# Key weights of a decoder's second memory: loaded by GpSimd's queue into eight buffers of the queries' ring and split by GpSimd in turn with ScalarE and VectorE

## The chip, the core and the metric

The kernel runs on one core of a Trainium2 chip. The time is the device time of one execution in microseconds (us). The core has TensorE (PE in the profile, with its weight loads as PEld), VectorE (DVE), ScalarE (ACT), GpSimd (POOL) and SyncE (SP), which in this kernel issues the DMAs. Each engine works through its own queue in order; an instruction waits at the head of its queue until the semaphores that it needs have been raised.

## What is computed

A decoder trunk of two layers over 1024 tokens of width 1024. Each layer projects its input, runs a main path (causal pooling in layer 0, forgetting attention in layer 1) and a cross-attention of 4 heads into 256 memory tokens, gates both, projects back and normalizes. The part that matters here is the cross-attention's keys and values, computed in both layers from the same memory tokens with each layer's own weights:

```
def memory_attention(q_mem, mem, w_mem_kv):
    mkv = mem @ w_mem_kv
    mk = mkv[..., :D_MEM].reshape(B, M, MEM_HEADS, MEM_HEAD_DIM)
    mv = mkv[..., D_MEM:].reshape(B, M, MEM_HEADS, MEM_HEAD_DIM)
    q = q_mem.reshape(B, S, MEM_HEADS, MEM_HEAD_DIM)
    logits = jnp.einsum('bshd,bmhd->bhsm', q, mk) * (MEM_HEAD_DIM ** -0.5)
    p = jax.nn.softmax(logits, axis=-1)
    return jnp.einsum('bhsm,bmhd->bshd', p, mv).reshape(B, S, D_MEM)

x = layer_norm(ALPHA * x + y, ln_g[layer], ln_b[layer])    # at the end of each layer
```

The second memory of the title is that of layer 1: same tokens, second set of weights.

## The kernel before

Products are made at nearly float32 precision from three products of parts. A float32 operand is split (`hi_lo`, L159) into a high part (fp32r, a copy by ScalarE, L162), a low part (bf16, source minus high, by VectorE, L163) and a top part (bf16, a copy by ScalarE, L164). `three` (L153) pairs them: high with high, top with low, low with top. `gp_hi_lo` (L166) makes the same three parts on GpSimd alone (L157, L168); in this kernel it is used in layer 1's attention (`low[0]`). A weight block of 128 x 512 is loaded into a buffer `raw` (a ring of 4) by SyncE and split into ring `w` (6 buffers, so 3 split blocks) by `split_w` (L171).

At the end of layer 0, `OutProj.rest` (L457) goes over four pairs of row blocks. For each pair it runs three product groups of 48 products (L441) in the order 2, 0, 1; group 2 reads weights that lie in the buffers "B" of the first pool `in0`, group 1 reads some that lie in its buffers "Y". `norm` (L481) then normalizes the two row blocks on VectorE (L490 to L503), stores them, and leaves eight transposes per row block in the list `turns`. `spread` (L301) lets TensorE run one of them between other products; each four fill a PSUM bank "T", from which `hi_lo` writes the layer's output X1 (buffers "A"), the input of layer 1.

Layer 1 begins with `mem_kv(1)` (L609). It loads the memory tokens in four blocks into `raw` and splits them into buffers "T". `mem_attention` (L309) then projects the four heads' keys at once (L313 to L315, `keys`, `project`, L238): 24 products of 128 x 256 for each head (L248), with the last transposes of layer 0 spread among them. Each head needs two halves of weights (pc = 0 and 1, 256 KB each), loaded and split by `split_w`. Odd heads take the parts in the order top, low, high, even heads in the order high, top, low. The products gather in one of two PSUM banks "pj", emptied by a `hi_lo` into `mk` (buffers "MK"). Then the first input slab of layer 1 follows (`slab`, L193, products L214).

The queries and, later, much else of layer 1 lie in the ring `xy` (L600): ten buffers "B" of 4 KB per partition in the second pool, `in1`. Pool `in1` is opened after `in0` is closed and takes over its space; within a pool the space is laid out in the order in which the tags are first asked for, in `in0` "Y" (4 buffers), "B" (8) and "W" (4). A buffer that takes over space waits for whatever last read or wrote it. The order of instructions in each queue is set when the program is built, by the framework's own scheduler, except where `manual_schedule` fixes TensorE's order (after the slabs of the memory attention, and in the main attention of layer 1).

Of the kernel before, what the change touches and what calls it, by code (L numbers as in the profile page):

```python
# [10 lines left out]
F32R = mybir.dt.float32r  # L11
BF16 = mybir.dt.bfloat16
# [6 lines left out]
P = 128  # L19
# [6 lines left out]
MH = 4  # L26
# [46 lines left out]
def trunk_kernel(ctx, tc, x, xT, memT, win, wk, wv0, wv, wmk, wmv, wout, poolw, pscale, lng, lnb, bforget, out):  # L73
# [5 lines left out]
    nc = tc.nc  # L79
# [14 lines left out]
    def nm(tag):  # L94
        count[0] += 1
        return f"{tag}{count[0]}"

    def sb(shape, tag, bufs, dt=F32, where=None):
        return (where or pool).tile(shape, dt, tag=tag, name=nm(tag), bufs=bufs)

    def ps(shape, tag, bufs):
        return psum.tile(shape, F32, tag=tag, name=nm(tag), bufs=bufs)
# [7 lines left out]
    def MK(shape, dt=F32R):  # L110
        return sb(list(shape), "MK", 4, dt)

    def raw(shape):
        return sb(list(shape), "raw", 4)
# [35 lines left out]
    def parts_of(make, shape):  # L150
        return Split(make(shape), make([shape[0], 2] + list(shape[1:]), BF16))

    def three(a, b):  # L153
        return (a.hi, b.hi), (a.top, b.lo), (a.lo, b.top)

    def gp_copy(to, src):
        nc.gpsimd.tensor_scalar(to, src, 1.0, 1.0, ALU.mult, ALU.mult)  # L157

    def hi_lo(to, src, pinned=False, top=None):  # L159

        pin = tc.keep_in_program_order if pinned else lambda ins: ins
        pin(nc.scalar.copy(to.hi, src))  # L162
        pin(nc.vector.tensor_tensor(to.lo, src, to.hi.bitcast(F32), ALU.subtract))  # L163
        (top or nc.scalar.copy)(to.top, src)  # L164

    def gp_hi_lo(to, src):  # L166
        gp_copy(to.hi, src)
        nc.gpsimd.tensor_tensor(to.lo, src, to.hi.bitcast(F32), ALU.subtract)  # L168
        gp_copy(to.top, src)

    def split_w(src_dram, shape):  # L171
        r = raw(shape)
        nc.sync.dma_start(r, src_dram)
        to = parts_of(wt, shape)
        (gp_hi_lo if low[0] else hi_lo)(to, r)
        return to
# [49 lines left out]
        nc.scalar.activation(dst, acc, AF.Tanh, scale=0.5)  # L226
        nc.vector.scalar_tensor_tensor(dst, dst, 1.0, acc, ALU.add, ALU.mult)

    def mem_kv(l):

        ms = [parts_of(T, [P, 4, NMEM]) for _ in range(2)]
        for q in range(4):
            r = raw([P, 2, NMEM])
            nc.sync.dma_start(r, memT[:, 2 * q : 2 * q + 2, :])
            hi_lo(ms[q // 2][:, 2 * (q % 2) : 2 * (q % 2) + 2, :], r)
        mk, projected = parts_of(MK, [P, MH, NMEM]), []

        def project(w_dram):  # L238

            acc = ps([P, NH], "pj", 2)[:, :NMEM]  # L240
            ws = [split_w(w_dram[pc], [P, 4, P]) for pc in range(2)]
            parts = (1, 2, 0) if len(projected) % 2 else (0, 1, 2)
            projected.append(acc)
            for i in parts:
                for pc in range(2):
                    w, m = three(ws[pc], ms[pc])[i]
                    for k in range(4):
                        nc.tensor.matmul(  # L248
                            acc, w[:, k, :], m[:, k, :],
                            start=(i, pc, k) == (parts[0], 0, 0), stop=(i, pc, k) == (parts[2], 1, 3),  # L250
                        )
                        if k % 3 == 0:
                            spread()
            return acc

        two, v = (MK([P, MH, 2 * 2, P], F16) for _ in range(2))
        undo = const.tile([P, 8], F32, tag="undo", name=nm("undo"), bufs=1)[:, :MH]

        def keys(h):
            hi_lo(mk[:, h, :], project(wmk[l, h]))  # L260

        def vals(h):
            scaled_halves(
                project(wmv[l, h]), [two[:, h, 2 * e : 2 * e + 2, :].rearrange("p m t -> p (m t)") for e in range(2)],
                undo[:, h : h + 1],
            )
            if h == MH - 1:
                nc.sync.dma_start_transpose(v.rearrange("p h b d -> p (h b) d"), two.rearrange("p h b t -> p (h b t)"))

        return (mk, v, undo), keys, vals  # L270

    def scaled_halves(u, halves, un, by_tile=lambda t: t):

        m, e, sc = (tiny(1) for _ in range(3))
        nc.vector.tensor_reduce(m, u, AX.X, ALU.max, apply_absolute_value=True)
        nc.vector.tensor_scalar(m, m, 2.0 ** -100, None, ALU.max)
        nc.vector.tensor_scalar(e.bitcast(I32), m.bitcast(I32), 0x7F800000, None, ALU.bitwise_and)
        nc.vector.reciprocal(sc, e)  # L280
        nc.vector.tensor_scalar(sc, sc, 2.0 ** 14, None, ALU.mult)
        nc.vector.tensor_scalar(un, e, 2.0 ** -15 / PSCALE, None, ALU.mult)
        (hi, lo), u = halves, by_tile(u)
        nc.scalar.activation(hi, u, AF.Copy, scale=sc)
        nc.vector.scalar_tensor_tensor(lo, u, sc, hi, ALU.mult, ALU.subtract)
# [15 lines left out]
    def spread():  # L301

        if turns:
            turns.pop(0)()
# [232 lines left out]
    with tc.tile_pool(name="in0", bufs=1) as in0:  # L537
# [47 lines left out]
        out_proj = OutProj(0, w_slots(wtags, in0), y0d)  # L585
        pool_group(0)
        kv = mem_kv(0)
        mem_attention(0, X, kv, bt, lambda: sb([P, S], "Y", 4, F32, in0), y0d[2])
        for g in range(1, 4):
# [8 lines left out]
    with tc.tile_pool(name="in1", bufs=1) as in1:  # L598
# [7 lines left out]
        def vt(shape, dt=F32R):  # L606
            return sb(shape, "V", 4, dt, in1)

        kv = mem_kv(1)  # L609
        mem_attention(1, X, kv, xy, lambda: vt([P, S], F32), y1d[2])  # L610
        cumd = dram.tile([HEADS, S], F32, name="cumd")
        fg = G((P, 8, ST * HEADS))
# [118 lines left out]
        def pair_units(p):  # L731

            yield from qk_units(p)
            if p >= 2:
                u = MK([P, S], F32)
                yield from slab(wv[p - 2], X, lambda cols, acc: nc.scalar.copy(u[:, cols], acc))
            pairs[p].append(first_vs[p] if p < 2 else values_of(u))
# [214 lines left out]
        with tc.manual_schedule(engines={PE}):  # L952
            own, following = pair_units(0), pair_units(1)
# [66 lines left out]
```

## Time and profile before

| | |
|---|---|
| median of 3 runs | 1219.99 us (1217.21 to 1220.11) |
| profiled execution | 1218.15 us, its span 1216.4 us |
| TensorE busy | 1193.7 us (98%) |
| VectorE busy | 793.3 us (65%) |
| ScalarE busy | 697.4 us (57%) |
| GpSimd busy | 221.0 us (18%), nothing between the load of x and 601 us |
| DMA | 178.68 MB, all loads and stores on one queue (q1), issued by SyncE |

The page shows one execution. Rows of a timeline have the start, the duration, the engine, the line, the operation and the tiles written and read; x is how many follow each other, and a bracket gives the idle time ahead and what ended it. Rows of a group have the count, then busy time and mean duration in ns, then the idle time before and what ended it. Rows of one tile have minimum, median and maximum. The mean granted clock is 0.997 of full speed.

### The profile page before, as it was taken

The numbers are of one execution on the slowest core, as the hardware profiler recorded it, in microseconds if no ns is written. First come the engines' busy times: TensorE is split into PE (matmuls) and PEld (weight loads), VectorE is DVE, ScalarE is ACT, GpSimd is POOL, SyncE is SP. The second block draws the span as 40 slices with busy tenths as digits, with TensorE's granted clock in tenths as the row PEclk, the third lists the DMA queues.
The fourth block names the chain that finished last, engine by engine and source line by source line (L and its number), as shares of the span: only waits on it lengthen the run. The fifth ranks groups of instructions, "written<-read, shape, count | busy, mean of one in ns | idle before, by whom it ended". The sixth has DMA issues, their size and how long they took to land. (4 is left out here: it accounts for less than half of the span.)

```text
span 1216.4 us, 20026 instructions
## 1 busy us (share of the span) xinstructions
PE 1193.7 (98%) x7018; PEld 758.7 (62%) x7018; DVE 793.3 (65%) x1853; ACT 697.4 (57%) x1474; POOL 221.0 (18%) x349
## 2 busy tenths in 40 slices
PE   9999999999999998999999999999999999999996
PEld 4566666555555666667686666666666666665553
DVE  7534676475644457357736888878877888874754
ACT  6556774374542345567533777767776777685220
POOL 4000000000000000000002454544444434640000
PEclk9999999999999999999999999999999999999999
DMA  6232553232452333234517879988887989895340
GB/s 229 84 112 95 122 131 139 95 121 88 164 182 104 111 129 116 70 96 109 159 52 181 162 161 194 181 187 172 182 195 159 193 188 229 222 241 195 132 156 36
DMA packets 267414, 178.68 MB, mean 147 GB/s; under 512 B 212272, under 2 KB 225712, under 8 KB 267312
## 3 DMA queue, kind: packets, MB, share of 16 engines
q1 hardware_dynamic: 267312, 177.40, 56.2%
q8 instruction: 55, 0.90, 0.3%
q14 instruction: 47, 0.39, 0.1%
HBM read 94.97 MB, written 22.61 MB: 97 GB/s over the span
## 5 line engine op out<-in xcount | busy, mean ns | idle before, releaser
L214 PE MATMUL pj<-A,w 128*128 128x512 bf16 (+1 forms) x2928 | 684.7, 390 | 3.1 <-DVE B L724 1.6
L214 PEld LDWEIGHTS <-w 128*128 128x128 bf16 x1984 | 182.3, 98 | 223.8 <-issue 23.3
L214 PEld LDWEIGHTS pj<-A,w 128*128 128x128 f32 x976 | 181.1, 189 | 45.8 <-ACT A L162 2.8
L789 ACT ACTIVATE T<-MK,s 128x512 f32<-128x512 f32 x192 | 111.3, 580 | 41.5 <-DVE s L781 23.6
L811 DVE SCALAR_TENSOR_TENSOR P<-T,s,P 128x512 f16<-128x512 f32 x192 | 111.6, 613 | 34.7 <-ACT P L810 33.4
L163 DVE TENSOR_TENSOR w<-raw,w 128x512 bf16<-128x512 f32 x106 | 75.6, 714 | 83.6 <-PE pj L214 51.5
L810 ACT ACTIVATE P<-T,s 128x512 f16<-128x512 f32 x192 | 103.0, 576 | 46.0 <-ACT T L789 20.1
L441 PEld LDWEIGHTS <-T 128*128 128x128 bf16 x736 | 70.7, 98 | 82.9 <-issue 3.7
L191 PE MATMUL L<-B,B 128*128 128x512 f32 (+3 forms) x384 | 105.8, 381 | 2.2 <-DVE s L781 2.1
L686 POOL MEMSET G<- 128x128 f32 x1 | 0.2, 208 | 581.5 <-ACT MK L164 581.5
L191 PEld LDWEIGHTS L<-B,B 128*128 128x128 f32 x384 | 70.8, 189 | 22.9 <-DVE s L781 4.8
L162 ACT CAST w<-raw 128x512 fp32r<-128x512 f32 x106 | 65.9, 621 | 26.6 <-PE pj L214 14.6
L157 POOL TENSOR_SCALAR w<-raw 128x512 fp32r<-128x512 f32 x108 | 67.3, 629 | 65.0 <-PE pj L214 59.7
L781 DVE CUSTOM_DVE_ANT_0 MK<-L,R 128x512 f32<-128x512 f32 (+3 forms) x128 | 72.5, 566 | 8.7 <-PE L L191 6.9
L164 ACT CAST w<-raw 128x512 bf16<-128x512 f32 x106 | 65.7, 620 | 18.9 <-PE pj L214 18.2
L773 POOL TENSOR_SCALAR_AFFINE_SELECT R<-R 128x128 f32<-128x128 f32 x128 | 41.3, 328 | 174.4 <-DVE s L781 129.4
L168 POOL TENSOR_TENSOR w<-raw,w 128x512 bf16<-128x512 f32 x54 | 69.6, 1288 | 18.7 <-PE pj L214 16.2
L163 DVE TENSOR_TENSOR T<-T,T 128x1024 bf16<-128x1024 f32 x23 | 28.0, 1218 | 52.2 <-ACT T L162 36.9
L833 PE MATMUL O<-T,V 128*64 128x128 f16 (+1 forms) x1152 | 57.6, 220 | 2.7 <-DMA T<-P 2.5
L833 PEld LDWEIGHTS <-V 128*64 128x64 f16 (+1 forms) x1152 | 50.2, 104 | 15.2 <-issue 5.7
L162 ACT CAST T<-T 128x1024 fp32r<-128x1024 f32 x23 | 24.1, 1046 | 60.3 <-DMA T<-y1d 33.9
L441 PE MATMUL pj<-B,T 128*128 128x512 bf16 (+1 forms) x192 | 52.6, 383 | 0.0
(230 smaller groups left out, 1699.3 us busy)
## 6 DMA issues: line engine op xcount, KB each, us to landing
raw<-in_win_dram SPq DMA_DIRECT2D x96, 256.0 KB, 2.8
raw<-in_wout_dram SPq DMA_DIRECT2D x40, 256.0 KB, 2.8
B<-B SPq DMA_DIRECT2D x32, 256.0 KB, 4.2
R<-cumd SPq DMA_DIRECT2D x16, 512.0 KB, 5.0
y0d<-Y SPq DMA_DIRECT2D x12, 512.0 KB, 3.1
T<-y0d SPq DMA_DIRECT2D x12, 512.0 KB, 3.8
T<-y1d SPq DMA_DIRECT2D x11, 512.0 KB, 4.9
raw<-in_wmk_dram SPq DMA_DIRECT2D x16, 256.0 KB, 2.6
```

The lines of the kernel that those rows point to most:

```text
L157: nc.gpsimd.tensor_scalar(to, src, 1.0, 1.0, ALU.mult, ALU.mult)
L162: pin(nc.scalar.copy(to.hi, src))
L163: pin(nc.vector.tensor_tensor(to.lo, src, to.hi.bitcast(F32), ALU.subtract))
L168: nc.gpsimd.tensor_tensor(to.lo, src, to.hi.bitcast(F32), ALU.subtract)
L191: nc.tensor.matmul(acc, a, b, start=i == 0, stop=i == len(terms) - 1)
L214: nc.tensor.matmul(accs[n], a[:, k, :], b[:, pc * 4 + k, n * NH : (n + 1) * NH], start=seen[n] == 1, stop=seen[n] == 3 * KT,)
L441: nc.tensor.matmul(accs[a][nh], y, w, start=kt == 8 and i == 0, stop=kt == 7 and i == 2,)
L781: nc.vector.tensor_tensor_reduce(p[:, lo:up], lg, R[:, lo:up], 1.0, top, ALU.add, ALU.min, m[:, n : n + 1])
L789: nc.scalar.activation(e, p[:, lo:up], AF.Exp, bias=top, scale=-1.0, accum_out=sums[:, n, hd % 2, i : i + 1],)
L810: nc.scalar.activation(pair[:, lo:up], e, AF.Copy, scale=r)
L811: nc.vector.scalar_tensor_tensor(pair[:, L + lo : L + up], e, r, pair[:, lo:up], ALU.mult, ALU.subtract)
L833: nc.tensor.matmul(acc[rows, (i % 4) * P : (i % 4) * P + P], v[:, b, 2 * j : 2 * j + (1 if e else 2), :].rearrange("p e d -> p (e d)"), pt ...
```

## The change

For layer 1 alone, `mem_kv` is given the ring `xy` (`own`). Three things change.

The top parts of the memory tokens are copied by GpSimd (`gp_copy`) instead of ScalarE.

The eight halves of key weights get buffers of their own: `ahead` takes eight buffers of ring `xy`, two for each head (one for the high parts of both halves, one for their low and top parts). They no longer pass through ring `w`. It is called before any key is projected. It loads the eight halves by GpSimd's queue in place of SyncE's, three loads ahead of the split, still through the four `raw` buffers.

Even halves are split by GpSimd alone (`gp_hi_lo`), odd halves by ScalarE (high), VectorE (low) and GpSimd (top). `keys` hands the split weights to `project`, which then loads none. The products and their number are the same.

```diff
-    def mem_kv(l):
+    def mem_kv(l, own=None):
 
         ms = [parts_of(T, [P, 4, NMEM]) for _ in range(2)]
         for q in range(4):
             r = raw([P, 2, NMEM])
             nc.sync.dma_start(r, memT[:, 2 * q : 2 * q + 2, :])
-            hi_lo(ms[q // 2][:, 2 * (q % 2) : 2 * (q % 2) + 2, :], r)
+            hi_lo(ms[q // 2][:, 2 * (q % 2) : 2 * (q % 2) + 2, :], r, top=gp_copy if l else None)
         mk, projected = parts_of(MK, [P, MH, NMEM]), []
 
-        def project(w_dram):
+        def ahead():
+
+            src = [wmk[l, h, pc] for h in range(MH) for pc in range(2)]
+            heads = [(own([P, 2, 4, P], F32R), own([P, 2, 2, 4, P], BF16)) for _ in range(MH)]
+            to = [Split(hi[:, pc], pair[:, pc]) for hi, pair in heads for pc in range(2)]
+            rs = []
+            for k in range(3 + len(src)):
+                if k < len(src):
+                    rs.append(raw([P, 4, P]))
+                    nc.gpsimd.dma_start(rs[k], src[k])
+                n = k - 3
+                if n >= 0 and n % 2:
+                    hi_lo(to[n], rs[n], top=gp_copy)
+                elif n >= 0:
+                    gp_hi_lo(to[n], rs[n])
+            return [to[2 * h : 2 * h + 2] for h in range(MH)]
+
+        def project(w_dram, ws=None):
 
             acc = ps([P, NH], "pj", 2)[:, :NMEM]
-            ws = [split_w(w_dram[pc], [P, 4, P]) for pc in range(2)]
+            ws = ws or [split_w(w_dram[pc], [P, 4, P]) for pc in range(2)]
...
+        early = ahead() if own else None
+
         def keys(h):
-            hi_lo(mk[:, h, :], project(wmk[l, h]))
+            hi_lo(mk[:, h, :], project(wmk[l, h], early and early[h]))
...
-        kv = mem_kv(1)
+        kv = mem_kv(1, xy)
```

In the built program the queues of all engines hold the same instructions in the same order as before outside this stretch, from the split of the memory tokens to the start of layer 1's first slab.

## The prediction

> **What bounds the kernel now.** I first read the page's engine totals, then its busy time by stretches, then TensorE's timeline where a stretch is not full.
>
> ```profile
> span 1216.4 us, 20026 instructions
> PE 1193.7 (98%) x7018; PEld 758.7 (62%) x7018; DVE 793.3 (65%) x1853; ACT 697.4 (57%) x1474; POOL 221.0 (18%) x349
> ```
>
> TensorE is busy 98% of the span, so a change elsewhere pays only where TensorE waits. Cut into 20 us, the only unfilled stretch of this neighbourhood is the one where layer 0 hands over to layer 1:
>
> ```profile
> 440.00:460.00 20.00, 20.00 (x98) 12.44 (x97) 8.20 (x13) 9.85 (x18) 0.00 (x0) 1.00 0.38 125
> 460.00:480.00 20.00, 16.05 (x111) 12.74 (x110) 17.07 (x37) 12.76 (x29) 0.00 (x0) 0.91 0.31 94
> 480.00:500.00 20.00, 20.00 (x113) 13.17 (x112) 7.96 (x18) 10.90 (x22) 0.00 (x0) 1.00 0.40 118
> ```
>
> Columns: stretch, length, busy time and count of PE, PEld, DVE, ACT, POOL, granted clock, DMA share, GB/s. From 460 to 480 TensorE idles 3.95 us, its clock averages 0.91, and GpSimd does nothing. TensorE's timeline there:
>
> ```profile
> 462.18 0.59 PE L441 MATMUL pj<-Y,T 128*128 128x512 bf16 x2
> 462.62 0.59 PE L441 MATMUL pj<-MK,T 128*128 128x512 bf16 x2
> 463.07 3.94 PE L248 MATMUL pj<-T,w 128*128 128x256 f32 x33
> 467.31 1.06 PE L294 MATMUL T<-ident,G 128*128 128x128 f32 x8 [0.29 <-DVE s L493]
> 470.99 1.65 PE L248 MATMUL pj<-T,w 128*128 128x256 f32 x7 [2.29 <-ACT w L162]
> 478.54 0.61 PE L248 MATMUL pj<-T,w 128*128 128x256 bf16 x4 [0.67 <-ACT w L164]
> 479.85 2.43 PE L248 MATMUL pj<-T,w 128*128 128x256 bf16 x20 [0.70 <-ACT w L164]
> 482.12 10.76 PE L214 MATMUL pj<-A,w 128*128 128x512 f32 x48
> 492.72 2.88 PE L248 MATMUL pj<-T,w 128*128 128x256 f32 x24
> 495.35 4.91 PE L214 MATMUL pj<-A,w 128*128 128x512 f32 x21
> ```
>
> The out-projection of layer 0 ends at 463.1, the 96 key products (L248) run until the first slab of layer 1 starts at 482.12: a stage of 19.05 us. Undisturbed, 24 such products take 495.35 - 492.72 = 2.63 us, 0.11 each, so 96 need 10.5 us, and the 16 transposes (8 in 1.06) 2.1 us. The stage thus holds 6.4 us that is not TensorE's work. That is the most the change can win. What ends the waits are ScalarE's splits of key weights (L162, L164); TensorE pays some more in the half clock behind the 2.29 us wait:
>
> ```profile
> 470.00:472.00 2.00, 1.01 (x6) 0.81 (x6) 2.00 (x5) 2.00 (x5) 0.00 (x0) 0.82 0.00 0
> 472.00:474.00 2.00, 2.00 (x11) 2.00 (x11) 1.65 (x3) 0.93 (x2) 0.00 (x0) 0.50 0.89 255
> 474.00:476.00 2.00, 2.00 (x16) 1.96 (x15) 1.48 (x3) 1.39 (x4) 0.00 (x0) 0.82 0.88 252
> ```
>
> **Part 1: when the new buffers may be written.** The eight buffers are the first of ring B in the second pool, whose space the first pool used. There tag Y was asked for before tag B, so the first four new buffers lie where Y lay. Those four Y buffers hold weights of the out-projection's last product group. In the built program GpSimd's first copy into a key buffer does wait for TensorE's last product that reads Y: the row at 462.18, whose second product ends at 462.77. So nothing is split ahead. Before, three of the eight halves lay ready in ring w by then:
>
> ```profile
> 444.45 0.69 DVE L163 TENSOR_TENSOR w<-raw,w 128x512 bf16<-128x512 f32 x1 [2.80 <-ACT w L162]
> 448.46 0.69 DVE L163 TENSOR_TENSOR w<-raw,w 128x512 bf16<-128x512 f32 x1 [1.17 <-ACT w L162]
> 453.63 0.68 DVE L163 TENSOR_TENSOR w<-raw,w 128x512 bf16<-128x512 f32 x1
> ```
>
> The last four new buffers lie over old B, free long before, but their writers stand behind the first ones in GpSimd's queue.
>
> **Part 2: GpSimd's chain.** In that queue, from 462.8: per head three copies and one subtraction (the even half whole, the odd half's top), with loads between. Durations, from the later layer where GpSimd splits the same shape:
>
> ```profile
> L168 POOL TENSOR_TENSOR w<-raw,w 128x512 bf16<-128x512 f32 x54 | 69.6, 1288 | 18.7 <-PE pj L214 16.2 <-POOL w L157 0.3
> L157 POOL TENSOR_SCALAR w<-raw 128x512 bf16<-128x512 f32 x54 | 34.3, 636 | 0.0
> L157 POOL TENSOR_SCALAR w<-raw 128x512 fp32r<-128x512 f32 x54 | 33.6, 622 | 65.0 <-PE pj L214 59.7 <-issue 5.1
> 674.83 1.28 POOL L168 TENSOR_TENSOR w<-raw,w 128x512 bf16<-128x512 f32 x1
> 676.07 0.62 POOL L157 TENSOR_SCALAR w<-raw 128x512 bf16<-128x512 f32 x1
> 676.64 0.29 POOL L773 TENSOR_SCALAR_AFFINE_SELECT R<-R 128x128 f32<-128x128 f32 x1
> ```
>
> Start to start a copy is 676.64 - 676.07 = 0.57 us, a subtraction 676.07 - 674.83 = 1.24. A head is 3 x 0.57 + 1.24 = 3.0 us; an even half 2.4.
>
> The first four loads take over the raw buffers of the memory tokens, whose last split on VectorE is
> ```profile
> 451.82 1.29 DVE L163 TENSOR_TENSOR T<-raw,T 128x512 bf16<-128x512 f32 x2 [2.66 <-PE T L294]
> ```
>
> so they are issued by about 455 and land under the out-projection. The other four reuse these buffers again and stand inside the chain: the fifth behind head 0, the sixth and seventh behind head 1, the eighth behind head 2's even half. What GpSimd pays for an issue no row shows; no load in this trace is GpSimd's. The nearest rows:
>
> ```profile
> 467.19 0.33 SPq L504 DMA_DIRECT2D x<-G  x1
> raw<-in_wmk_dram SPq DMA_DIRECT2D x16, 256.0 KB, 2.6
> ```
>
> Lower end: SyncE's 0.33 us for an issue. Upper end: 2.6, the whole load, as if GpSimd stood still until it landed. Between them I take 1.0, the mean of GpSimd's own copy (0.62) and subtraction (1.29), since it must do the issue as work of its own. The Trainium skill, "DMA: Bandwidth & Descriptors", section "Latency and other measured facts", puts about 1 us before the first byte for GpSimd's software path against about 0.6 for SyncE's; with an estimate of 1 us per issue its sum would be the same.
>
> So the eighth load is issued from 462.8 + 3.0 + 1.0 + 3.0 + 2 x 1.0 + 2.4 = 474.2, and lands 1.0 + 2.6 later, at 477.8.
>
> **Part 3: who waits for it.** ScalarE's queue in the built program then holds: the high copy of that load, the copy of the last-but-one transposed block, then the top part of head 0's keys, which frees TensorE's bank pj for head 2. Rows:
>
> ```profile
> 475.58 0.62 ACT L164 CAST w<-raw 128x512 bf16<-128x512 f32 x1
> 474.60 0.59 ACT L162 CAST A<-T 128x512 fp32r<-128x512 f32 x1 [0.48 <-PE T L294]
> 477.06 0.40 ACT L164 CAST MK<-pj 128x256 bf16<-128x256 f32 x1
> ```
>
> That is 0.62 + 0.59 + 0.40 = 1.6, so head 2 starts at 479.4; heads 2 and 3 are 48 products, 5.3 us. The first slab starts at 484.7 instead of 482.12: **+2.6 us**. GpSimd's last piece (head 3's odd top, behind the issue, head 2's odd top and head 3's even half: 474.2 + 1.0 + 0.6 + 2.4 + 0.6 = 478.8) is ready before head 3 needs it, and the last norm's output, held back on VectorE by the split of the sixth load, is transposed near 477: neither is last. With 0.33 per issue the same sum gives 484.7 - 4 x 0.67 = 482.0, no change; with 2.6 it gives 484.7 + 4 x 1.6 = 491.1, +9.
>
> **Part 4: GpSimd beside VectorE.** VectorE is at its fullest here (17.07 of 20). GpSimd's copies elsewhere are longer where VectorE subtracts at the same time:
>
> ```profile
> L157 POOL TENSOR_SCALAR MK<-B x2: 613/835/1057, 1046.9 to 1048.5; 128x512 bf16<-128x512 f32 x2
> L157 POOL TENSOR_SCALAR A<-T 128x1024 bf16<-128x1024 f32 x7 | 11.8, 1707 | 1.5 <-DMA T<-in_xT_dram 1.5
> ```
>
> A disturbed copy is 1.06 against 0.61, 0.44 of the 0.69 of a VectorE subtraction, 64% of it. While GpSimd's chain runs to 474.2, VectorE has such operations (two large inputs, neither from a product): one scale of 1.27, two of 0.74, three key splits of 0.69, 4.8 us:
>
> ```profile
> 465.89 1.27 DVE L503 SCALAR_TENSOR_TENSOR G<-G,s,P 128x1024 f32<-128x1024 f32 x1
> 467.55 0.74 DVE L501 SCALAR_TENSOR_TENSOR G<-G,s,P 128x512 f32<-128x512 f32 x1
> ```
>
> Lower end 0 (as if they never met), upper end 4.8 (each holds GpSimd up for its whole length). I take 64%, **+3.1 us**. The Trainium skill, "SBUF — State Buffer", section "Who interferes with whom", says that a VectorE instruction with two SBUF inputs and a GpSimd one that reads SBUF fully block each other; that speaks against this change, and by it the sum is nearer the upper end, an estimate of +2.6 + 4.8 = +7.4. The 1707 ns copy above agrees with it.
>
> **Part 5: what is taken away.** ScalarE loses the tops of the memory tokens (4 x 0.62) and of all key weights and half the high parts; VectorE loses half the subtractions. From 440 to 463 TensorE was full, so this frees nothing on the path; in the stage it is what made the 3.95 us of waiting, and the sum above already lets ScalarE start at once. Half clock: the trace lost 2 x (0.18 + 0.50 + 0.18) = 1.7 us to it (the three rows of 2 us above); the new waits of TensorE (near 474 to 476 and 477 to 479) are like the old one, so I change nothing, with -1.7 to +1.7 for the range. After the first slab the queues hold the same instructions in the same order as before, so what the stage loses is not won back: TensorE is full.
>
> **Sum.** +2.6 + 3.1 = **+5.7 us**. The profiled execution took 1218.15 us (span 1216.4), which would become 1223.9; it lies 1.84 under the median of 1219.99, to which I add the same: **1225.7**.
>
> **The rivals.** (a) Cheap: issues cost 0.33 and GpSimd is not disturbed. For it: 54 subtractions of GpSimd average 1288 ns beside a busy VectorE. Against it: the disturbed copies above. With both the sum is 0; with one alone it is +2.6 or +3.1: 1220 to 1223. (b) The change does what its words say: the weights lie ready at 463, and only TensorE's work is left. For it: GpSimd idle, the space of old B free. Against: the wait on Y. Up to -6.4, 1213.6; half of it is 1216.8. (c) GpSimd stands still until each load lands, 2.6 per issue: +9 and with disturbance to +14, 1229 to 1234. For it: nothing; against: SyncE's own queue shows an issue at 0.33 and a landing at 2.6 apart. It decides from about 2 us per issue.
>
> **Chances.** The forecast's own case, +3.7 to +9: 0.64; (a) 0.25; (b) 0.05; (c) 0.06. The bound of what can be told from no change is 0.3%, 3.7 us: slower 0.64 + 0.06 = 0.70, the same 0.25, faster 0.05. The range leaves out (b), the part of (a) in which the half clock is won back too, and most of (c): lower end 1219.5, half a microsecond under no change; upper end 1219.99 + 2.6 + 4.8 + 4 x 0.3 (an issue at 1.3) + 1.7 = 1230.3, about 1231.
>
> **What would show it.** Right: GpSimd's first key copy starts at 462.8, not near 441; the first slab starts near 487.8; ScalarE's split of the eighth load ends the wait before head 2; GpSimd's copies of the first two heads exceed 0.62; its gaps at the loads are about 1 us. Wrong: key copies before 463, or a first slab before 484.

## The result, and the profile after

The changed kernel takes 1226.18 us (median of 6 runs, 1225.18 to 1227.65); six runs of the kernel before, beside them, have a median of 1218.88 us. The ratio is 1.0061, 95% interval 1.0048 to 1.0074: slower by 7.3 us, where +5.7 was forecast. The profiled execution took 1225.53 us. The page's totals after:

```profile
span 1223.8 us, 20029 instructions
PE 1196.5 (98%) x7018; PEld 760.2 (62%) x7018; DVE 795.5 (65%) x1849; ACT 688.6 (56%) x1458; POOL 243.3 (20%) x377
```

The span grew by 7.4 us. TensorE's timeline of the stage after (in the changed file the out-projection's product is L460, the key product L265, the transpose L313):

```profile
462.79 0.59 PE L460 MATMUL pj<-Y,T 128*128 128x512 bf16 x2
463.22 0.59 PE L460 MATMUL pj<-MK,T 128*128 128x512 bf16 x2
...
464.14 1.67 PE L265 MATMUL pj<-T,B 128*128 128x256 f32 x12 [0.22 <-POOL B L157]
466.56 1.05 PE L265 MATMUL pj<-T,B 128*128 128x256 bf16 x8 [0.74 <-POOL B L157]
469.31 0.61 PE L265 MATMUL pj<-T,B 128*128 128x256 bf16 x4 [1.71 <-POOL B L157]
472.00 0.39 PE L265 MATMUL pj<-T,B 128*128 128x256 bf16 x1 [2.07 <-POOL B L157]
472.19 1.91 PE L313 MATMUL T<-ident,G 128*128 128x128 f32 x8
...
479.96 0.63 PE L313 MATMUL T<-ident,G 128*128 128x128 f32 x4 [1.43 <-ACT w L162]
481.52 1.08 PE L313 MATMUL T<-ident,G 128*128 128x128 f32 x4 [0.94 <-DVE G L522]
482.26 6.72 PE L265 MATMUL pj<-T,B 128*128 128x256 f32 x48
488.82 1.55 PE L214 MATMUL pj<-A,w 128*128 128x512 f32 x6
```

The out-projection ends at 463.22 + 0.59 = 463.81 (463.21 before) and the first slab of layer 1 starts at 488.82 (482.12 before). The stage between took 25.0 us instead of 18.9: +6.1 of the 7.4. The other 1.3 lies half ahead of it (0.6) and half behind it (1223.8 - 488.82 = 735.0, against 734.3).

The brackets give what TensorE waited: 0.22 + 0.74 + 1.71 + 2.07 + 1.43 + 0.94 = 7.11 us, against 3.95 before: +3.2. The rest shows in the granted clock. Busy time by stretches of 2 us (columns as before, the granted clock is the third number from the end):

```profile
472.00:474.00 2.00, 2.00 (x10) 1.93 (x11) 0.00 (x0) 0.69 (x2) 1.98 (x4) 0.50 0.39 78
474.00:476.00 2.00, 2.00 (x11) 1.36 (x10) 2.00 (x3) 1.48 (x3) 1.49 (x2) 0.50 0.46 184
476.00:478.00 2.00, 2.00 (x12) 1.66 (x10) 2.00 (x7) 0.59 (x1) 1.24 (x3) 0.55 0.52 135
...
480.00:482.00 2.00, 1.06 (x7) 0.85 (x8) 2.00 (x4) 1.30 (x3) 1.85 (x2) 0.80 0.38 70
482.00:484.00 2.00, 2.00 (x11) 1.98 (x9) 1.98 (x5) 1.47 (x5) 0.00 (x0) 0.50 0.75 282
484.00:486.00 2.00, 2.00 (x17) 1.64 (x17) 1.25 (x2) 2.00 (x5) 0.00 (x0) 0.85 0.84 274
```

Counted as in the prediction, over the stretches that TensorE filled, 2 x (0.50 + 0.50 + 0.45 + 0.50 + 0.15) = 4.2 us are lost to the half clock, against 1.7 before: +2.5. The stretch from 480 to 482, about half of it busy, adds at most 2 x 0.20 = 0.4. Waits and clock together make 5.7 to 6.1 of the 6.1.

Who is late shows in the other queues. GpSimd's timeline after:

```profile
463.48 1.19 POOL L157 TENSOR_SCALAR B<-raw 128x512 fp32r<-128x512 f32 x2 [7.81 <-PE pj L460]
464.65 1.27 POOL L168 TENSOR_TENSOR B<-raw,B 128x512 bf16<-128x512 f32 x1
...
466.45 0.59 POOL L247 DMA_DIRECT2D raw<-in_wmk_dram  x1
467.08 2.18 POOL L157 TENSOR_SCALAR B<-raw 128x512 fp32r<-128x512 f32 x2
469.23 1.69 POOL L168 TENSOR_TENSOR B<-raw,B 128x512 bf16<-128x512 f32 x1
470.89 1.05 POOL L157 TENSOR_SCALAR B<-raw 128x512 bf16<-128x512 f32 x1
471.89 1.14 POOL L247 DMA_DIRECT2D raw<-in_wmk_dram  x2
...
476.73 0.60 POOL L247 DMA_DIRECT2D raw<-in_wmk_dram  x1 [1.24 <-DVE s L516]
```

The first key copy waits 7.81 us for the out-projection's last product that reads "Y" (462.79 + 0.59 = 463.38). Head 0 then passes at the forecast durations; head 1's copies and subtraction (467.08 to 471.9) are longer. An issue costs 0.59. VectorE's timeline after, in the same stretch:

```profile
468.77 2.70 DVE L520 SCALAR_TENSOR_TENSOR G<-G,s,P 128x512 f32<-128x512 f32 x2
474.00 0.16 DVE L515 RECIPROCAL s<-s 128x1 f32<-128x1 f32 x1 [2.54 <-ACT s L514]
474.08 1.96 DVE L163 TENSOR_TENSOR B<-raw,B 128x512 bf16<-128x512 f32 x1
...
476.15 0.67 DVE L163 TENSOR_TENSOR A<-T,A 128x512 bf16<-128x512 f32 x1
...
478.53 2.84 DVE L522 SCALAR_TENSOR_TENSOR G<-G,s,P 128x512 f32<-128x512 f32 x2
```

Of the scales, which took 0.74 each, one pair takes 2.70 and the other 2.84, and a key subtraction 1.96 instead of 0.69; the subtraction with one input in a PSUM bank ("A<-T,A") keeps its 0.67. ScalarE's timeline after:

```profile
473.28 0.59 ACT L162 CAST A<-T 128x512 fp32r<-128x512 f32 x1 [6.75 <-PE T L313]
473.76 0.21 ACT L514 ACTIVATE s<-s 128x1 f32<-128x1 f32 x1
...
479.83 0.63 ACT L162 CAST B<-raw 128x512 fp32r<-128x512 f32 x1
...
481.74 0.37 ACT L164 CAST MK<-pj 128x256 bf16<-128x256 f32 x1 [0.53 <-DVE MK L163]
```

Read together, the four queues show a ring of waits. GpSimd is late with head 1's parts, so TensorE stands still 1.71 us and, from 469.9 to 472.0, another 2.07. The transposes of layer 0's output (472.19) stand behind those products in TensorE's queue. ScalarE waits 6.75 us for them, and the last norm's square root (L514, 473.76) stands behind that copy. VectorE waits 2.54 us for the square root, and GpSimd's eighth issue waits 1.24 us for VectorE. Head 2 starts at 482.26, behind the last transposes (481.52) and when ScalarE has emptied head 0's bank (481.74 + 0.37 = 482.11). Both had waited for VectorE, whose last two scales end at 478.53 + 2.84 = 481.37.

### The profile page after: what moved, and what is told of

Read it like the earlier page. It is cut to its first block, busy times and chain, and to the rows that moved or that the text cites. A ratio compares the mean times of both kernels' runs of the same rounds, so it can differ in the third digit from the quotient of the medians.

```text
span 1223.8 us, 20029 instructions
## 1 busy us (share of the span) xinstructions
PE 1196.5 (98%) x7018; PEld 760.2 (62%) x7018; DVE 795.5 (65%) x1849; ACT 688.6 (56%) x1458; POOL 243.3 (20%) x377
## 5 line engine op out<-in xcount | busy, mean ns | idle before, releaser
L460 PEld LDWEIGHTS <-T 128*128 128x128 bf16 x736 | 70.7, 98 | 82.8 <-issue 3.7
L163 DVE TENSOR_TENSOR w<-raw,w 128x512 bf16<-128x512 f32 x98 | 70.1, 715 | 76.0 <-PE pj L214 51.1
L157 POOL TENSOR_SCALAR T<-raw 128x512 bf16<-128x512 f32 x4 | 3.6, 918 | 428.7 <-PE pj L460 428.7
L162 ACT CAST w<-raw 128x512 fp32r<-128x512 f32 x98 | 60.8, 620 | 21.3 <-PE pj L214 14.1
L164 ACT CAST w<-raw 128x512 bf16<-128x512 f32 x98 | 60.7, 619 | 18.7 <-PE pj L214 18.1
L460 PE MATMUL pj<-B,T 128*128 128x512 bf16 (+1 forms) x192 | 52.7, 383 | 0.0
```

The source lines that it names most:

```text
L460: nc.tensor.matmul(accs[a][nh], y, w, start=kt == 8 and i == 0, stop=kt == 7 and i == 2,)
```

## The experiments

All kernels below are timed beside runs of the kernel before on the same chip. "First slab" is the time from VectorE's first subtraction for the memory tokens, which lies ahead of everything the change touches, to the first slab, less the same in the kernel before (482.12 - 440.36 = 41.76 us). The column comes from the one profiled execution of each kernel, the times from all its runs. In kernels without GpSimd's split the lines are two lower than after (L458, L263, L311).

| kernel | median us | ratio to before, 95% interval | first slab |
|---|---|---|---|
| the change | 1226.18 | 1.0061 (1.0048 to 1.0074) | +6.1 |
| before, token tops on GpSimd | 1218.48 | 0.9998 (0.9989 to 1.0007) | +0.8 |
| change, loads by SyncE | 1225.84 | 1.0059 (1.0046 to 1.0071) | +6.3 |
| change, GpSimd splits nothing | 1224.01 | 1.0043 (1.0030 to 1.0055) | +3.6 |
| both of these | 1223.66 | 1.0042 (1.0028 to 1.0056) | +3.2 |
| change, first pool's ring | 1221.04 | 1.0022 (1.0013 to 1.0031) | +3.5 |
| the same, GpSimd makes tops only | 1219.51 | 1.0006 (0.9997 to 1.0015) | -0.5 |
| the same, GpSimd splits nothing | 1219.34 | 1.0009 (1.0000 to 1.0018) | -0.4 |
| the same, and loads by SyncE | 1215.69 | 0.9974 (0.9965 to 0.9983) | -4.1 |
| the same, token tops by ScalarE too | 1215.45 | 0.9979 (0.9970 to 0.9987) | -3.8 |
| first pool's ring, all halves by GpSimd | 1227.20 | 1.0059 (1.0045 to 1.0072) | +6.6 |

The theory at the start was that of the prediction: nothing can be split before the out-projection ends, and then GpSimd's chain, with its loads, lands the eighth half late. The rivals were contention with VectorE, and the price of the place of the buffers by itself.

**One part alone: the memory tokens' tops on GpSimd.** The kernel before, with this one line.

```diff
-            hi_lo(ms[q // 2][:, 2 * (q % 2) : 2 * (q % 2) + 2, :], r)
+            hi_lo(ms[q // 2][:, 2 * (q % 2) : 2 * (q % 2) + 2, :], r, top=gp_copy if l else None)
```

> The kernel before the change with only the top parts of the memory tokens copied by GpSimd. Theory: these four copies lie under the out-projection, where TensorE is full: no change, within 1 us of before. Rival A (GpSimd's copies hold VectorE up wherever they are): +1 us or more.

The ratio is 0.9998: this part is neither gain nor loss.

**The change with its loads issued by SyncE.**

```diff
-                    nc.gpsimd.dma_start(rs[k], src[k])
+                    nc.sync.dma_start(rs[k], src[k])
```

> The change with its eight key loads issued by SyncE again, nothing else. Theory: GpSimd's chain loses four issues of 0.6 us, so the first slab comes about 2.4 us earlier than in the change, and the kernel is still 4 to 6 us slower than before the change. Rival B (the loads by GpSimd's queue are what costs): within 1 us of the kernel before the change. Rival A (GpSimd blocking VectorE): no gain over the change, +6 to +8 us.

The time stays (1.0059 against 1.0061). The end of GpSimd's chain, in its timeline of this kernel:

```profile
477.84 0.61 POOL L157 TENSOR_SCALAR B<-raw 128x512 bf16<-128x512 f32 x1
```

TensorE's last waits and the first slab, in its timeline:

```profile
479.43 1.15 PE L313 MATMUL T<-ident,G 128*128 128x128 f32 x8 [2.61 <-ACT A L164]
481.62 7.26 PE L265 MATMUL pj<-T,B 128*128 128x256 f32 x48 [1.04 <-ACT MK L164]
488.72 1.55 PE L214 MATMUL pj<-A,w 128*128 128x512 f32 x6
```

GpSimd is done at 478.45, 3.4 us earlier than with its own loads (481.86), and the slab still starts at 488.72. So neither the issues nor the landing of the eighth half set the end; the theory's -2.4 us did not come. What remains, by these rows, is the ring of waits through transposes and the norm: before head 2 TensorE waits for ScalarE, which empties the transposes' bank (A) and head 0's bank (MK).

**The change without any split on GpSimd.** All halves go through ScalarE and VectorE; the place and the loads stay.

```diff
-                if n >= 0 and n % 2:
-                    hi_lo(to[n], rs[n], top=gp_copy)
-                elif n >= 0:
-                    gp_hi_lo(to[n], rs[n])
+                if n >= 0:
+                    hi_lo(to[n], rs[n])
```

> The change with all eight halves split by ScalarE and VectorE (16 copies and 8 subtractions), loads still by GpSimd's queue into the second pool's ring. Theory: nothing is ready at 463 either, ScalarE then has 16 copies of 0.52 us start to start, 8.3 us, besides its 8 copies of the transposed blocks, 4.2 us, and the 8 key copies, 2.4 us: 15 us in all, so the stage is 19 to 22 us long, the kernel 0 to +3 us against before the change and 4 to 7 us faster than the change; VectorE's scales keep 0.74 and 1.27 us. Rival A (GpSimd blocking VectorE is all of the loss): equal to before the change. Rival C (the early buffers do not matter, GpSimd's split is only slow): also equal to before.

It is 2.2 us faster than the change, less than the 4 to 7 expected, and still 0.43% slower than before, so both rivals, which had it equal to before, are out. GpSimd's split costs something, but not most.

**The place alone.** The last edit together with the loads by SyncE: only the eight buffers in the second pool are left of what could cost.

> The change with its eight buffers in the second pool, but loads by SyncE and every half split by ScalarE and VectorE: only the place of the buffers is left of what cost time. It differs from the best version so far only in the pool. Theory (the second pool's first write waits for the out-projection's last product at 463, so eight halves must be split by ScalarE and VectorE inside the stage, where the kernel before had three ready): 1.5 to 5 us slower than before, 1220.5 to 1224, first key split at about 463.5, first slab 2 to 4 us late; it stands 5 to 8 us above the kernel with the first pool's ring. Rival (the loss without GpSimd's splits, +5.2 us, came from loads queued behind GpSimd, and the pool itself costs nothing): within 1.2 us of before.

The theory holds: 1.0042, slab 3.2 us late. ScalarE's timeline of this kernel has the wait that GpSimd's had in the change:

```profile
464.34 0.62 ACT L162 CAST B<-raw 128x512 fp32r<-128x512 f32 x1 [1.10 <-PE pj L458]
...
478.07 1.06 ACT L164 CAST A<-T 128x512 bf16<-128x512 f32 x2
```

TensorE's timeline of the same kernel:

```profile
478.69 1.77 PE L311 MATMUL T<-ident,G 128*128 128x128 f32 x8 [4.15 <-ACT A L164]
480.56 6.48 PE L263 MATMUL pj<-T,B 128*128 128x256 f32 x48
486.88 5.47 PE L214 MATMUL pj<-A,w 128*128 128x512 f32 x23
```

The first key split comes at 464.34, behind the out-projection's last product that reads "Y". Eight halves then fill ScalarE inside the stage, the copies of the transposed blocks stand behind them (478.07), and TensorE waits 4.15 us for their bank.

**The change with the first pool's ring.** The call moves to the end of the first pool's block and takes that pool's ring B, free since the last pair's product group 2, which ends near 441 us.

```diff
         out_proj.rest(x, X1, x1)
+        kv = mem_kv(1, bt)
...
-        kv = mem_kv(1, xy)
```

> The early weights go into ring B of the first pool (eight buffers, free when product group 2 of the last pair of row blocks ends, near 441 us) in place of the second pool's; all else as in the change. Theory (the change loses because nothing is split before the last product that reads Y, and the splits then queue on GpSimd): GpSimd's first key copy comes near 446 us instead of 463.5, all eight halves are ready near 464, the stage from the last out-projection product to the first slab shrinks from 25.2 us (19.1 before the change) to 13 to 15, and the kernel is 4 to 6 us faster than before the change. Rival A (GpSimd's work itself costs, by blocking VectorE wherever it runs): the norm is held up in its new place too, the kernel stays 2 to 5 us slower than before the change. Rival B (the loads by GpSimd's queue are what costs): no better than the change, +6 to +8 us.

GpSimd's first key copy now starts at 446.17 and its last split is done at 465.83, as the theory had it, but the kernel is 0.22% slower than before, not 4 to 6 us faster. VectorE's timeline of this kernel has the reason, a subtraction pair of 6.33 us (5.73 for the first alone) with the norm's first eviction (here L509) behind it:

```profile
460.64 6.33 DVE L163 TENSOR_TENSOR B<-raw,B 128x512 bf16<-128x512 f32 x2 [2.38 <-ACT B L162]
466.90 0.67 DVE L509 SCALAR_TENSOR_TENSOR G<-G,L 128x512 f32<-128x512 f32 x1
```

From 459.84 to 465.83 GpSimd ran eight instructions without a pause. TensorE then waited 4.42 us for the norm's evictions, which free its banks.

**Less of GpSimd, in the first pool's ring.** First only its top copies are left to it, then no part of the keys but the loads.

```diff
-                if n >= 0 and n % 2:
+                if n >= 0:
                     hi_lo(to[n], rs[n], top=gp_copy)
-                elif n >= 0:
-                    gp_hi_lo(to[n], rs[n])
```

> e1 with GpSimd doing only the top copy of every half, ScalarE all high parts and VectorE all low parts. Theory (a run of GpSimd work without a gap is what starves VectorE): GpSimd now runs at most two copies between loads, so VectorE's subtractions are stretched by at most about 1.2 us each instead of 5, the first slab starts 14 to 17 us after the out-projection's last product, 2 to 5 us faster than before the change. Rival A' (any GpSimd copy beside VectorE costs as much as in e1): +1 to +3 us against before.

> As e1 (early weights in ring B of the first pool), but all eight halves split by ScalarE and VectorE; loads still by GpSimd's queue. Theory, as it stands after e1 to e4 (two causes: nothing is ahead in the second pool; and a run of GpSimd copies keeps VectorE's subtraction from SBUF waiting, 6.33 us for two in e1, with the norm behind it): no VectorE subtraction of 128 x 512 exceeds 0.75 us while the out-projection runs, TensorE's 4.4 us wait for VectorE of e1 is gone, the first slab starts 13 to 16 us after the out-projection's last product, and the kernel is 3 to 6 us faster than before the change. Rival D (ScalarE and VectorE cannot take the splits under the out-projection without holding up the blocks of the running norm): no better than e1, +2 us or more against before.

The second kernel has the edit of the third experiment instead. Both give the time of the kernel before (1.0006 and 1.0009), so the expected gains of 2 to 6 us are missing in both. Without GpSimd's split no subtraction of the keys on VectorE is over 0.69, but TensorE still waits 1.23 and 2.77 us for VectorE; with GpSimd's tops these waits are 2.12 and 1.17, and single subtractions take up to 1.15. So the next suspect was the loads.

**And the loads by SyncE.** The one-line edit shown above.

> e5 with the eight key loads issued by SyncE. Theory (who issues the loads does not matter, as in e2): within 1.5 us of e5. Rival B (GpSimd's issue costs, but was covered in e2): 2 us or more faster than e5.

0.9974: faster than both kernels, and the rival that blamed the loads is right. With loads by GpSimd the norm's first eviction (L507 on VectorE) starts at 461.37; by SyncE:

```profile
459.39 0.69 DVE L163 TENSOR_TENSOR B<-raw,B 128x512 bf16<-128x512 f32 x1 [0.35 <-ACT B L162]
460.00 0.68 DVE L507 SCALAR_TENSOR_TENSOR G<-G,L 128x512 f32<-128x512 f32 x1
```

In GpSimd's queue an issue stands behind the tokens' tops and its own waits; ScalarE's last three loads' splits begin 1.4 to 2.0 us earlier when SyncE loads. In the second pool the same edit did nothing, which fits that nothing there is split before 463, when the first four loads have landed. GpSimd's splits with loads by SyncE were not run in the first pool's ring.

**And the tokens' tops by ScalarE again**, so that nothing is left for GpSimd.

```diff
-            hi_lo(ms[q // 2][:, 2 * (q % 2) : 2 * (q % 2) + 2, :], r, top=gp_copy if l else None)
+            hi_lo(ms[q // 2][:, 2 * (q % 2) : 2 * (q % 2) + 2, :], r)
```

> Early weights in the first pool's ring B, loaded by SyncE, split by ScalarE and VectorE, and now also the memory tokens' top parts by ScalarE as before the change: nothing is left for GpSimd here. Theory (GpSimd's only remaining part, four token tops of 0.6 us near 440 to 453, lies far ahead of the norm and of the first slab): 1215.7 within 2 us, ratio 0.996 to 0.999 against the kernel before, first slab within 1 us of the kernel with tops on GpSimd. Rival A (the tops stretch VectorE's token splits, 2.12 us for two, and that delay reaches the norm): 1 to 2 us faster still, 1213.5 to 1215. Rival B (ScalarE, with four more copies of 0.62, becomes late for the key splits): 1 to 3 us slower, 1217 to 1219.

0.9979, the same within the intervals: what wins is the early split into the first pool's buffers, and GpSimd has no part in it. TensorE's timeline of this kernel, the fastest by its median:

```profile
464.05 2.96 PE L263 MATMUL pj<-T,B 128*128 128x256 f32 x24
468.91 2.50 PE L263 MATMUL pj<-T,B 128*128 128x256 bf16 x21 [1.90 <-DVE s L515]
```

One wait of 1.90 us is left, now for the norm on VectorE and not for key weights, and the granted clock is 1.00 from 460 to 480.

**All eight halves by GpSimd, in the first pool's ring.** It tests whether GpSimd's run as such keeps VectorE waiting.

```diff
-                if n >= 0 and n % 2:
-                    hi_lo(to[n], rs[n], top=gp_copy)
-                elif n >= 0:
+                if n >= 0:
                     gp_hi_lo(to[n], rs[n])
```

> Early weights in the first pool's ring B, loaded by GpSimd, all eight halves split by GpSimd alone: VectorE and ScalarE have no part of the early keys. GpSimd's chain is 8 x (2.4 + 0.6) = 24 us, from 446 to 470, so weights come at 452, 458, 464 and 470 and hold up TensorE at most before the last head. Theory (a run of GpSimd instructions without a gap keeps a VectorE instruction with two SBUF inputs waiting, as it did with 6.33 us for two subtractions of the alternating split; instructions with an input from a PSUM bank aren't touched): no VectorE subtraction of raw minus high for keys is left to be starved, but the norm's scales (1.27 and 0.74 alone) and the w splits that fall before 470 take 2 to 6 us, the evictions L507 and the splits from bank T keep 0.7; time 1218 to 1222. Rival A (the long subtractions came from the interplay of VectorE's key splits with GpSimd's, and not from GpSimd's run as such): scales keep 1.27 and 0.74, VectorE is ahead of the other versions, slab at least 4 us earlier than before, 1213 to 1216. Rival B (GpSimd becomes the bound): TensorE waits for B by GpSimd before heads 2 and 3, 1222 to 1227.

The time, 1227.2, lies just above the range of rival B, but not for its reason: no wait of TensorE is for GpSimd's parts. GpSimd's timeline of this kernel, the end of its run:

```profile
469.83 1.19 POOL L157 TENSOR_SCALAR B<-raw 128x512 fp32r<-128x512 f32 x2
471.00 1.25 POOL L168 TENSOR_TENSOR B<-raw,B 128x512 bf16<-128x512 f32 x1
```

VectorE's timeline of the same stretch:

```profile
468.50 4.30 DVE L163 TENSOR_TENSOR w<-raw,w 128x512 bf16<-128x512 f32 x1 [8.10 <-ACT w L162]
472.72 0.67 DVE L507 SCALAR_TENSOR_TENSOR G<-G,pj 128x512 f32<-128x512 f32 x1
```

A single subtraction that takes 0.69 alone took 4.30 and ended half a microsecond after GpSimd's run did (471.00 + 1.25 = 472.25), while GpSimd's own instructions kept their length. TensorE waited 9.47 us for L507, the eviction behind it. The mechanism of the theory is there; its size was too small, since the 8.10 us in the bracket come on top: the `raw` buffers were in the hands of GpSimd's loads, so that the first slab's weights landed late (ScalarE waited 8.77 us for them) and VectorE's queue stood at their split.

## Why the prediction was right, and where its steps were not

**The total.** +7.3 against +5.7, inside the range; the time itself came nearer (1226.18 against 1225.7) because the kernel before ran 1.1 us faster beside it than in the runs shown first; that nearness is chance. The next steps say how much of that rests on the right reasons.

**Step 1, nothing is split ahead: right, and the largest part.** GpSimd's first key copy starts at 463.48, behind the last product that reads "Y", not near 441. With the place as the only cost the kernel loses 0.42%, where the change loses 0.61%, and the same kernel with the first pool's ring is 0.26% faster than before: the place decides the sign. The 0.42 is not a plain share of the 0.61, since without GpSimd's split ScalarE is the engine that is late. The reason given was imprecise. In the built program only four of the eight buffers lie over "Y" (one of head 0, one of head 2, both of head 3) and not the first four; yet the first write to any of them waits for the last use of the whole first pool. Laying another tag over "Y" leaves the same wait in the built program, and was not tried on the chip.

**Step 2, GpSimd's chain: the sum near, its terms not.** From the first copy to the eighth issue it took 476.73 - 463.48 = 13.25 us, where 11.4 was worked out. The three issues in between cost 0.59 + 1.14 = 1.73 instead of 3.0: the 1.0 taken was too much, and 0.59 lies between the bounds of 0.33 and 2.6. A wait of 1.24 us for VectorE was not foreseen. Copies and subtractions took 10.28 instead of 8.4, longer by 1.9, nearly all of it in head 1.

**Step 3, the eighth half ends the wait before head 2: wrong.** ScalarE does split it late (479.83), and head 2 starts at 482.26, as 479.4 + 3.1 would have it. But with loads by SyncE, where the step's own sum gives no more than the contention, the slab starts at the same time. The step put the last norm's transposes near 477 and called them not last. They started at 481.52, and head 2 stands behind them and behind head 0's bank, both held by VectorE's scales; with loads by SyncE it waits for that bank alone (1.04 us). Without GpSimd's split it is another queue: the transposes wait for ScalarE (4.15 us in the rows above). The step overlooked that the last transposes stand behind head 1's products in TensorE's queue, and the square root behind their copy in ScalarE's. So the +2.6 had about the right size by luck, for another cause: in the two kernels without GpSimd's split the slab is 3.2 to 3.6 late.

**Step 4, contention: right in kind, and one-sided.** Taking GpSimd's split away, as a whole, brings the slab 6.1 - 3.6 = 2.5 us forward with loads by GpSimd and 6.3 - 3.2 = 3.1 with loads by SyncE, beside the +3.1 forecast. This holds GpSimd's slowness too, so the contention alone isn't measured. The forecast counted only what GpSimd loses, and up to the eighth issue that was 1.9 of the 3.1, with 0.9 more behind it. VectorE lost more: the rows above have 2.70 + 2.84 for four scales of 0.74 and 1.96 for a subtraction of 0.69, which is 2.70 + 2.84 + 1.96 - 4 x 0.74 - 0.69 = 3.85 us. The Trainium skill, "SBUF — State Buffer", section "Who interferes with whom", has VectorE instructions with two SBUF inputs contend with GpSimd's reads, and those with at most one not: the trace agrees on both (1.96 for "B<-raw,B", 0.67 for "A<-T,A"). With the place alone, where GpSimd splits nothing, VectorE's key subtractions are back at 0.69 at most, and its last pair of scales at half the time:

```profile
472.84 1.41 DVE L520 SCALAR_TENSOR_TENSOR G<-G,s,P 128x512 f32<-128x512 f32 x2
```

That VectorE pays too could be read before the change. The copies of 128x1024 of the load of x, which the prediction showed beside its price, run beside VectorE's subtractions:

```profile
9.08 10.74 POOL L157 TENSOR_SCALAR A<-T 128x1024 bf16<-128x1024 f32 x6 [0.18 <-DMA T<-in_xT_dram]
13.98 1.52 DVE L163 TENSOR_TENSOR w<-raw,w 128x512 bf16<-128x512 f32 x1
```

A subtraction of 0.69 alone took 1.52 there.

**Step 5, half clock unchanged: wrong.** It cost 2.5 us more, outside the 1.7 allowed. There are two bouts of it instead of one, behind the wait of 2.07 and behind those of 1.43 and 0.94; the 48 last products took 488.82 - 482.26 = 6.56 us instead of 5.3. So the sum held partly by luck: the waits grew by 3.2, not by 5.7, and the half clock, put at no change, made up for it. That nothing is won back after the slab was right (735.0 against 734.3).

**The rivals.** (a) is out: cheap issues (loads by SyncE) don't make it cheap, and GpSimd is disturbed (1.9 us). (b) is what the change could have been: with the weights ready at 463 the slab came 3.8 to 4.1 us earlier, of the 6.4 at most. (c) is out by the 0.59 us of an issue.

## What to carry to other kernels

Before weights are moved ahead in time, ask what must happen before the first write to the new buffers. Here a ring of the next pool made "ahead" begin where the old pool ended, and the same loads and splits into a ring of the running pool turned 0.4% of loss into 0.2 to 0.3% of gain. An idle GpSimd is no free help beside a VectorE that works on two SBUF inputs: count what VectorE loses as well, and follow each queue past the engine that is late, since here the loss went through TensorE's, ScalarE's and VectorE's queues before it came back to TensorE.

## What the runs showed of the hardware that was not expected

A run of GpSimd instructions without a pause can hold a VectorE instruction with two SBUF inputs until the run ends, and not for one instruction only: one subtraction of 0.69 took 4.30 us with all halves on GpSimd, and one took 5.73 with the alternating split in the first pool's ring; both were over half a microsecond after GpSimd's last. The section of the Trainium skill cited above lets the engine that issues first hold the other for its instruction; here GpSimd's next instruction went first again, several times over. It does not always: earlier in the same alternating split two subtractions (447.35 and 453.93) took 1.81 and 1.69 and came in ahead of a GpSimd copy, which took 1.05 instead of 0.61. What decides between the two was not found.

A load issued by GpSimd occupied its queue for 0.55 to 0.60 us (the first one 0.73), against 0.33 for SyncE's issue.
